# Snapshot of product 1 moved to the second accumulation bank, and half of the low parts to VectorE, in a folded feed-forward block

## The chip, the cores and the metric

The kernel runs on one core of a Trainium2 chip. The metric is device time in microseconds, the median of several runs. The engines are named as in the profile: PE (TensorE, matmuls), PEld (its weight loads, which overlap), DVE (VectorE), ACT (ScalarE), POOL (GpSimd) and SP (SyncE, which issues most DMAs here). Each engine works through its own queue in order; an instruction that waits for a semaphore holds back everything behind it on that engine.

## The reference

One step of a decoder layer on 520 tokens (512 of a new sequence and 8 single ones), all in fp32:

```python
def _swiglu(x, wg, wu, wd):
    return (jax.nn.silu(x @ wg) * (x @ wu)) @ wd

h = h + 0.5 * _swiglu(_rms_norm(h, ffn1_norm), ffn1_w_gate, ffn1_w_up, ffn1_w_down)   # FFN1
m, ... = _hybrid_mixer(_rms_norm(h, mix_norm), ...)     # pooling, convolution, SSD scan
h = h + m
h = h + 0.5 * _swiglu(_rms_norm(h, ffn2_norm), ffn2_w_gate, ffn2_w_up, ffn2_w_down)   # FFN2
return _rms_norm(h, final_norm), ...                    # and the new states
```

The model width is 1024, the hidden width of each feed-forward block 2816 = 22 x 128. Only FFN1 is touched by the change.

## The kernel before, in words

**Precision.** Each fp32 operand is split into a high part (`hi`, a cast on ACT to the type that TensorE multiplies) and a low rest (`lo` = x - hi). A product of two operands is three matmuls (`mm3`, lines 133, 136 and 137: hi.hi, hi.lo, lo.hi). A low part of weights is made in one of two ways: on DVE as one subtraction from the raw weights (`split` and `part`), or by `part_by_dma` (lines 218 to 220): ACT casts hi, ACT writes -hi into lo, and a DMA issued on POOL adds the raw weights from DRAM onto it.

**Seven products.** The token dimension is split into two halves of 260 and the weights into 2 x 2 blocks, and the four block products of a tile are replaced by seven products of sums (a fast scheme of the Strassen kind). `sums` builds the weight sums s1 (line 396) and s2 (lines 397 and 398) on DVE, each 128 x 1024, and splits them into `shi`/`slo` (c from s1, d from s2; casts at line 121, low parts at line 123). Products 1 and 2 use the plain weights `whi`/`wlo`, products 7 and 5 the c sums, 6 and 3 the d sums, and product 4 the quarter `qhi`/`qlo` (512 columns). One product is 4 x 3 = 12 matmuls of 128 x 128 by 128 x 260, and a tile of 7 products has 84.

**PSUM.** Each tile has one bank `A` and a pair of banks `BE`, both with two buffers. Products 1, 6, 7 and 4 run into `A`, each but the first on top of what is there; between them ACT takes snapshots of the running sum into SBUF (`ac`, line 456: product 1 to a[0], 6 to a[1], 7 to c[0]). Products 5 and 3 run into BE[1] (product 5 also is snapshotted, to c[1]), product 2 alone into BE[0]. `gates` then adds BE and a (line 473, 128 x 520), multiplies by the rms factor r (line 474), applies silu on ACT (line 475) and multiplies by the other half (line 476); `close` (line 488) uses A after product 4, and `keep_g` (lines 332 to 340) makes the pair sums of two gate tiles and splits them for the down projection.

**The stream.** `stream` runs over tiles 2 to 21 of gate and up weights, and after tiles 8 and 16 over four down tiles each (`Down(c, d)`): 28 tiles. Per tile it loads the raw weights (2 x 512 KB on SP, into `raw`, two buffers), makes the parts, and issues product 1, then product 4 and the close of the tile before, then 5, 6, 3, 7, 2 (tiles 2 and 21: 2, 5, 6, 3, 7), then `gates`. The plain weights `whi`/`wlo` and the sums' parts have two buffers each, the quarter one. In tiles 4 to 21 and in the down tiles wlo is made by `part_by_dma`; the quarter of tiles 2 to 20 too.

**What sets the order.** The kernel is written for a framework that orders each engine's instructions itself by its own estimate, respecting dependencies. Only where the code says so is the written order kept: `keep_in_program_order` on the first matmul of a product (`pin`; before the change product 7 of tile 2 and product 1 of tile 3), and `queued(...)`, which sets an instruction behind another. Elsewhere the products of neighbouring tiles interleave: product 5 of a tile before product 4 of the one before, for example, and product 2 before product 7. Buffers come free by semaphores, whole tile by whole tile.

After the stream comes a last down projection of tiles 16 to 21, then the mixer and FFN2, which is not folded in this way and keeps its own code paths.

Of the kernel before, what the change touches and what calls it, by code (L numbers as in the profile page):

```python
# [10 lines left out]
F32 = mybir.dt.float32  # L11
F32R = mybir.dt.float32r
AF = mybir.ActivationFunctionType
ALU = mybir.AluOpType
# [49 lines left out]
def tile_trunk_step(ctx: ExitStack, tc: tile.TileContext, ins: dict, outs: dict):  # L64
# [27 lines left out]
    def queued(*ins):  # L92
        stack = ExitStack()
        for i in ins:
            stack.enter_context(tc.issue_after(i))
        return stack
# [120 lines left out]
    def part_by_dma(hi, lo, s, home):  # L217
        nc.scalar.copy(hi, s)
        nc.scalar.activation(out=lo, in_=hi.bitcast(F32), func=AF.Copy, scale=-1.0)
        nc.gpsimd.dma_start(out=lo, in_=home, accum_op=ALU.add)  # L220
# [22 lines left out]
    class Ffn:  # L243
# [4 lines left out]
        def __init__(self, nx, i, wx, gp, direct):  # L248
            self.nx, self.i, self.wx, self.gp, self.direct = nx, i, wx, gp, direct
            self.states = None  # L250
            self.folded = CHUNKS[0] + CHUNKS[1] if i == 1 else 0
            self.held = {} if self.folded else {CHUNKS[0] + 1: None, CHUNKS[0] + CHUNKS[1] + 1: None}
            self.dram, self.gs, self.pairs, self.few, self.later = {}, {}, {}, [], []
            self.w, self.A, self.BE, self.ac, self.g, self.tg, self.raw, self.banks, self.behind, self.plain_kept = (
                {} for _ in range(10)
            )
# [98 lines left out]
        def load(self, f, first, then, by_dma):  # L355
            i, wx, src = self.i, self.wx, ins[f"w{self.i}gu"]
            n = f"{i}_{f}"
            raw = raw_pair(n)
            if isinstance(f, int):
                drams = [src[2 * f + u] for u in range(2)]  # L360
            else:
                lo = f.c * CHUNKS[0]
                drams = [ins[f"w{i}d"][2 * f.d + u, :, lo * P : (lo + 8) * P] for u in range(2)]
            self.dram[f] = drams
            for u in range(2):
                nc.sync.dma_start(out=raw[:, u], in_=drams[u])
            with queued(*first):
                if self.folded and (f, 0) not in LOW_ON_DVE:
                    d1 = weight_homes(1024, f"{n}a", wp, 3, ("whi", "wlo"))
                    part_by_dma(*d1, raw[:, 0], drams[0])  # L370
                else:
                    d1 = split(raw[:, 0], 1024, f"{n}a", wp, 3, ("whi", "wlo"))
            with queued(*then, *(ends if by_dma and i == 1 else ())):
                self.sums(f, n, src, raw, d1, by_dma)
# [39 lines left out]
        def quarter(self, f, src):  # L414
            n = f"{self.i}_{f}b"
            if self.folded:
                hi, lo = (self.wx.tile([P, 512], F32R, tag=t, name=f"{t}_{n}") for t in ("qhi", "qlo"))
                h, l = hi, lo
                if len(src.shape) == 3:
                    h, l = (t.rearrange("p (j c) -> p j c", j=4) for t in (hi, lo))  # L420
                if isinstance(f, int) and (f, 1) not in LOW_ON_DVE:
                    home = self.dram[f][1]
                    home = home[:, 512:] if isinstance(f, int) else home.rearrange("p (j q c) -> p q j c", q=2, c=P)[:, 1]
                    part_by_dma(h, l, src, home)
                else:
                    part(h, l, src)
                self.w[f][4] = (hi, lo), range(4)
                return
            self.w[f][4] = split(src, 512, n, wp, 3, ("whi", "wlo")), range(4)

        def product(self, f, p):
            js = range(KD // 2)
            if f not in self.A:
                self.load(f, *self.behind.get(f, ((), (), False)))
                n = f"{self.i}_{f}"
                self.A[f] = ps[0].tile([P, 512], F32, tag="A", bufs=2, name=f"A{n}")
                self.BE[f] = ps[0].tile([P, 2, 512], F32, tag="BE", bufs=2, name=f"BE{n}")
                self.ac[f] = [self.wx.tile([P, 2, HB], F32, tag="ac", bufs=3, name=f"ac{n}_{q}") for q in range(2)]
            if p != 1 and 4 not in self.w[f]:
                self.quarter(f, self.held[f])  # L440
            slot, dst, opens = {1: (0, 0, True), 2: (1, 1, True), 5: (3, 2, True), 6: (5, 0, False),
                                3: (2, 2, False), 7: (4, 0, False), 4: (6, 0, False)}[p]
            out = self.A[f] if dst == 0 else self.BE[f][:, dst - 1]
            (whi, wlo), k = self.w[f][p]
            xth, xtl = self.nx[:2]
            for j in js:
                if isinstance(f, int):
                    x = xth[:, j, slot], xtl[:, j, slot]
                else:
                    x = (self.gs[f.c * CHUNKS[0] // 2 + j][:, q, {5: 6, 6: 5}.get(slot, slot)] for q in range(2))  # L450
                mm3(out[:, :HB], ws(whi, k[j]), ws(wlo, k[j]), *x, opens and j == 0,
                    j == KD // 2 - 1, pin=j == 0 and (f, p) in ((2, 7), (3, 1)), skip_group_check=True)
            a, c = self.ac[f]
            keep = {1: a[:, 0], 6: a[:, 1], 7: c[:, 0], 5: c[:, 1]}.get(p)
            if keep is not None:
                nc.scalar.copy(keep, out[:, :HB])  # L456
            if p == 7:
                nc.vector.tensor_tensor(out=c[:, 0], in0=c[:, 0], in1=c[:, 1], op=ALU.add)

        def gates(self, f):  # L460
            if not isinstance(f, int):
                td = self.nx[2].rearrange("p (b t) -> p b t", b=2)
                r = self.nx[3].rearrange("p (b t) -> p b t", b=2)
                hd = h[:, 2 * f.d].rearrange("p (b t) -> p b t", b=2)
                a, c = self.ac[f]
                nc.vector.tensor_tensor(out=td, in0=self.BE[f][:, :, :HB], in1=a, op=ALU.add)
                nc.vector.scalar_tensor_tensor(out=td, in0=td, scalar=-0.5, in1=r, op0=ALU.mult, op1=ALU.mult)
                nc.vector.tensor_tensor(out=hd, in0=td, in1=hd, op=ALU.add)
                nc.vector.scalar_tensor_tensor(out=c[:, 1], in0=c[:, 0], scalar=0.5, in1=r[:, 1], op0=ALU.mult,
                                               op1=ALU.mult)  # L470
                return
            tg = self.tg[f] = self.gate_home(f)
            nc.vector.tensor_tensor(out=tg, in0=self.BE[f][:, :, :HB], in1=self.ac[f][0], op=ALU.add)
            nc.vector.tensor_tensor(out=tg, in0=tg, in1=self.nx[3].rearrange("p (b t) -> p b t", b=2), op=ALU.mult)
            nc.scalar.activation(out=tg, in_=tg, func=AF.Silu)
            nc.vector.tensor_tensor(out=tg[:, 1], in0=self.ac[f][1][:, 0], in1=tg[:, 1], op=ALU.mult)

        def close(self, f):
            if not isinstance(f, int):
                r = self.nx[3].rearrange("p (b t) -> p b t", b=2)  # L480
                hd = h[:, 2 * f.d + 1].rearrange("p (b t) -> p b t", b=2)
                c = self.ac[f][1]
                nc.vector.scalar_tensor_tensor(out=c[:, 0], in0=self.A[f][:, :HB], scalar=0.5, in1=r[:, 0],
                                               op0=ALU.mult, op1=ALU.mult)
                nc.vector.tensor_tensor(out=hd, in0=c, in1=hd, op=ALU.add)
                return
            tg = self.tg[f]
            nc.vector.tensor_tensor(out=tg[:, 0], in0=self.A[f][:, :HB], in1=tg[:, 0], op=ALU.mult)
            self.keep_g(f, tg)
# [4 lines left out]
        def stream(self, before, last_chunk):  # L494
# [6 lines left out]
            for t in tiles:  # L501
                self.product(t, 1)
                if prev is not None:
                    self.product(prev, 4)
                    self.close(prev)
                for p in (2, 5, 6, 3, 7) if t in (2, KF - 1) else (5, 6, 3, 7, 2):
                    self.product(t, p)
                self.gates(t)
                if t == 3:
                    with queued(*ends[1:]):  # L510
                        self.later.pop()()
                prev = t
# [150 lines left out]
    room = [*ffn1.cells("x2"), *ffn1.cells("x1"), *ffn1.cells("x0")]  # L663
    spare = [t.bitcast(F32) for t in ffn1.cells("sq")]
    sqs = spare.pop().rearrange("p (a b) t -> p a (b t)", a=2)
    ffn1.pairs[2] = spare.pop()

    def cell1(name):
        return room.pop().bitcast(F32)
# [723 lines left out]
```

## Time and profile before

| | before |
| --- | --- |
| time, median of 3 runs | 991.24 us (986.99, 991.24, 991.29) |
| profiled execution, its own time | 986.47 us |
| its span | 984.5 us, mean granted clock 0.995 |
| PE busy | 966.0 us (98%) |
| DVE busy | 815.6 us (83%) |
| ACT busy | 605.4 us (61%) |
| POOL busy | 125.7 us (13%) |
| moved by DMA | 135.18 MB, of it 29.63 MB on POOL's queue |

The time of the profiled execution is 2 us longer than its span, which begins and ends with the first and last instruction recorded. Matmuls are pipelined: a matmul row lasts 0.28 us, but the next one starts 0.12 us later, so a "busy" PE need not be one at its peak; the count of matmuls in a stretch tells more than the busy time. In the rows, `[1.75 <-ACT ac L456]` means that the engine was idle for 1.75 us before the instruction, and that an ACT instruction of line 456 on `ac` ended it. `SPq` and `POOLq` are DMA queues. A number behind a tile's name is its tile in the stream, and a letter the part: a plain, b quarter, c and d the two sums.

### The profile page before, as it was taken

How to read it: one execution, taken by the hardware profiler on the slowest of the kernel's cores; microseconds unless marked ns; L12 is line 12 of the kernel's file. 1: busy time of each engine (PE TensorE's matmuls, PEld its weight loads, DVE VectorE, ACT ScalarE, POOL GpSimd, SP SyncE). 2: the span in 40 equal slices, each digit the busy share in tenths (PEclk: the TensorE clock that was granted, in tenths of full speed). 3: DMA queues.
4: the chain of work that ended last, by engine and by line, in shares of the span. 5: the costliest groups of instructions: out<-in, count | busy, mean ns of one | idle time of the engine just before them, and what ended most of it. 6: DMA issues, size and time to landing. Idle time of an engine off the chain costs nothing.

```text
span 984.5 us, 19586 instructions
## 1 busy us (share of the span) xinstructions
PE 966.0 (98%) x7772; PEld 944.8 (96%) x7772; DVE 815.6 (83%) x1340; ACT 605.4 (61%) x1112; POOL 125.7 (13%) x206
## 2 busy tenths in 40 slices
PE   9999999999999999999999999999999999999996
PEld 8899999999989999999999999999999999999995
DVE  6898987888877688879978897999967899667886
ACT  7778657777557465485776675666643566514663
POOL 0011101111111000056341000100012000110010
PEclk9999999999999999999999999999999999999998
DMA  7577666776567232253334232523346423462232
GB/s 208 162 187 175 150 169 164 169 196 150 133 175 175 97 124 87 92 195 129 108 139 158 73 137 87 154 101 129 115 119 187 160 89 126 123 176 80 86 119 87
DMA packets 50459, 135.18 MB, mean 137 GB/s; under 512 B 7288, under 2 KB 15416, under 8 KB 50368
## 3 DMA queue, kind: packets, MB, share of 16 engines
q1 hardware_dynamic: 39840, 104.18, 30.8%
q0 software_dynamic: 10256, 29.63, 15.7%
q8 instruction: 61, 1.00, 0.4%
q14 instruction: 30, 0.25, 0.1%
q10 hardware_dynamic: 272, 0.13, 0.0%
HBM read 126.57 MB, written 7.34 MB: 136 GB/s over the span
## 4 chain that ended last, share of the span: by engine, by line
PE 78%; DVE 7%; DMA 7%; ACT 4%; issue 3%; SPq 0%; DVEq 0%; ACTq 0%
PE A L133 7%; PE A L136 7%; PE A L137 7%; PE BE L137 5%; PE BE L136 5%; PE BE L133 5%; PE P L282 4%; PE dn L137 4%; PE dn L136 4%; PE dn L133 4%; DMA raw<-in_w1gu 4%; PE wo L133 2%; PE wo L137 2%; PE wo L136 2%; PE inx L133 2%
## 5 line engine op out<-in xcount | busy, mean ns | idle before, releaser
L137 PE MATMUL dn<-g,wlo_2d 128*128 128x260 f32 x256 | 72.5, 283 | 0.0
L133 PE MATMUL dn<-g,whi_2d 128*128 128x260 f32 x256 | 72.1, 282 | 0.0
L136 PE MATMUL dn<-g,whi_2d 128*128 128x260 f32 x256 | 72.1, 282 | 0.0
L396 DVE TENSOR_TENSOR s<-raw 128x1024 f32<-128x1024 f32 x39 | 47.6, 1220 | 22.0 <-DMA raw<-in_w1gu 18.8
L456 ACT COPY ac<-A 128x260 f32<-128x260 f32 x123 | 44.0, 372 | 17.7 <-PE A L137 16.9
L133 PEld LDWEIGHTS dn<-g,whi_2d 128*128 128x128 f32 x256 | 48.2, 188 | 0.0
L136 PEld LDWEIGHTS dn<-g,whi_2d 128*128 128x128 f32 x256 | 48.2, 188 | 0.0
L137 PEld LDWEIGHTS dn<-g,wlo_2d 128*128 128x128 f32 x256 | 48.1, 188 | 0.0
L582 DVE SCALAR_TENSOR_TENSOR td<-dn,r_f 128x520 f32<-128x520 f32 (+1 forms) x25 | 16.8, 675 | 32.5 <-PE dn L137 32.5
L1121 POOL DMA_DIRECT2D out_nss<-hs x16 | 8.7, 545 | 259.1 <-DVE hs L1119 259.0
L121 ACT CAST whi_2d<-raw_2d 128x1024 fp32r<-128x1024 f32 (+1 forms) x18 | 18.5, 1026 | 36.8 <-PE dn L136 15.0
L133 PE MATMUL wo<-catg,whi_wo 128*128 128x260 f32 x128 | 37.1, 290 | 0.0
L133 PE MATMUL inz<-xh_mx,whi_inz 128*128 128x260 f32 x128 | 36.6, 286 | 0.0
L133 PE MATMUL inx<-xh_mx,whi_inx 128*128 128x260 f32 x128 | 36.4, 284 | 0.0
L137 PE MATMUL wo<-catg,wlo_wo 128*128 128x260 f32 x128 | 36.3, 283 | 0.0
L136 PE MATMUL inz<-xl_mx,whi_inz 128*128 128x260 f32 x128 | 36.2, 283 | 0.0
L137 PE MATMUL inz<-xh_mx,wlo_inz 128*128 128x260 f32 x128 | 36.2, 283 | 0.0
L136 PE MATMUL inx<-xl_mx,whi_inx 128*128 128x260 f32 x128 | 36.1, 282 | 0.0
L137 PE MATMUL inx<-xh_mx,wlo_inx 128*128 128x260 f32 x128 | 36.1, 282 | 0.0
L136 PE MATMUL wo<-catg,whi_wo 128*128 128x260 f32 x128 | 36.1, 282 | 0.0
L968 DVE SCALAR_TENSOR_TENSOR A<-U,h,A 128x544 f32<-128x544 f32 x36 | 28.8, 801 | 2.2 <-ACT A L966 1.8
L1117 ACT ACTIVATE so<-br,sxdt 128x128 f32<-128x128 f32 x64 | 20.4, 391 | 16.3 <-DMA br<-scr_bc 9.6
(2135 smaller groups left out, 4384.1 us busy)
## 6 DMA issues: line engine op xcount, KB each, us to landing
raw<-in_w2gu SPq DMA_DIRECT2D x44, 512.0 KB, 4.4
raw<-in_w1gu SPq DMA_DIRECT2D x41, 512.0 KB, 5.4
raw_2d<-in_w2d SPq DMA_DIRECT2D x16, 512.0 KB, 4.6
raw_wo<-in_w_out SPq DMA_DIRECT2D x12, 512.0 KB, 4.4
ab<-scr_acs SPq DMA_DIRECT2D x8, 512.0 KB, 3.7
h<-in_state_ssm SPq DMA_DIRECT2D x16, 256.0 KB, 3.2
raw_inz<-in_w_in SPq DMA_DIRECT2D x8, 512.0 KB, 4.4
hs<-in_state_ssm POOLq DMA_DIRECT2D x16, 256.0 KB, 3.4
```

Source lines behind the costliest of these rows:

```text
L121: cast = nc.scalar.copy(h, src)
L133: first = nc.tensor.matmul(ps, whi, xhi, start=start, stop=False, **kw)
L136: nc.tensor.matmul(ps, whi, xlo, start=False, stop=False, **kw)
L137: nc.tensor.matmul(ps, wlo, xhi, start=False, stop=stop, **kw)
L282: mm = nc.tensor.matmul(self.banks[f, u][b][:, :HB], ws(self.raw[f][:, u], j + 4 * q), xg[:, slot[q]], start=j == q == 0, stop=j == 3 and ...
L396: nc.vector.tensor_tensor(out=s1, in0=diag, in1=up0, op=ALU.add)
L456: nc.scalar.copy(keep, out[:, :HB])
L582: nc.vector.scalar_tensor_tensor(out=o, in0=s, scalar=-0.5, in1=q, op0=ALU.mult, op1=ALU.mult)
L968: nc.vector.scalar_tensor_tensor(out=A[:, :n], in0=U[:, j : j + n], scalar=w(j), in1=A[:, :n], op0=ALU.mult, op1=ALU.add)
L1117: nc.scalar.activation(out=o[:, q], in_=br, func=AF.Copy, scale=sxdt[:, j, b : b + 1]))
L1121: tc.keep_in_program_order(nc.gpsimd.dma_start(out=outs["nss"][:, b, 4 * g : 4 * g + 4], in_=hs))
```

## The change

Three things are edited, all for FFN1.

1. *Snapshot.* In all tiles but tile 2, the snapshot of product 1 is copied by ACT from bank A into bank BE[0] instead of into SBUF, and product 2 then accumulates on top of it, where before it opened the bank. The sum of BE and a in `gates` is then only needed in the second half (260 columns instead of 520) and is written in place in PSUM; the product with r reads from there.
2. *Low parts.* In tiles 4 to 21 the first 512 columns of wlo are subtracted on DVE; ACT and the accumulating DMA make only the second 512 columns. The quarter is made by the DMA only up to tile 6; from tile 7 on it is subtracted on DVE. The down tiles stay as they are.
3. *Order.* The first matmul of every product of FFN1 is pinned to the written order. The close of the tile before is issued after the first product of this tile that follows product 4, and silu is issued with the close, behind the last snapshot copy issued. The kept gates of an early tile (`later`) are closed at tile 5 instead of 3, and pair 4 gets a home in a spare cell.

```diff
--- before.py
+++ after.py
@@ -248,6 +248,7 @@
         def __init__(self, nx, i, wx, gp, direct):
             self.nx, self.i, self.wx, self.gp, self.direct = nx, i, wx, gp, direct
             self.states = None
+            self.whole = (2,)
             self.folded = CHUNKS[0] + CHUNKS[1] if i == 1 else 0
             self.held = {} if self.folded else {CHUNKS[0] + 1: None, CHUNKS[0] + CHUNKS[1] + 1: None}
             self.dram, self.gs, self.pairs, self.few, self.later = {}, {}, {}, [], []
@@ -367,7 +368,13 @@
             with queued(*first):
                 if self.folded and (f, 0) not in LOW_ON_DVE:
                     d1 = weight_homes(1024, f"{n}a", wp, 3, ("whi", "wlo"))
-                    part_by_dma(*d1, raw[:, 0], drams[0])
+                    hi, lo = d1
+                    n2 = 512 if isinstance(f, int) else 0
+                    nc.scalar.copy(hi, raw[:, 0])
+                    nc.scalar.activation(out=lo[:, n2:], in_=hi[:, n2:].bitcast(F32), func=AF.Copy, scale=-1.0)
+                    nc.gpsimd.dma_start(out=lo[:, n2:], in_=drams[0][:, n2:], accum_op=ALU.add)
+                    if n2:
+                        nc.vector.tensor_tensor(out=lo[:, :n2], in0=raw[:, 0, :n2], in1=hi[:, :n2].bitcast(F32), op=ALU.subtract)
                 else:
                     d1 = split(raw[:, 0], 1024, f"{n}a", wp, 3, ("whi", "wlo"))
             with queued(*then, *(ends if by_dma and i == 1 else ())):
@@ -418,7 +425,7 @@
                 h, l = hi, lo
                 if len(src.shape) == 3:
                     h, l = (t.rearrange("p (j c) -> p j c", j=4) for t in (hi, lo))
-                if isinstance(f, int) and (f, 1) not in LOW_ON_DVE:
+                if isinstance(f, int) and f <= 6 and (f, 1) not in LOW_ON_DVE:
                     home = self.dram[f][1]
                     home = home[:, 512:] if isinstance(f, int) else home.rearrange("p (j q c) -> p q j c", q=2, c=P)[:, 1]
                     part_by_dma(h, l, src, home)
@@ -440,6 +447,7 @@
                 self.quarter(f, self.held[f])
             slot, dst, opens = {1: (0, 0, True), 2: (1, 1, True), 5: (3, 2, True), 6: (5, 0, False),
                                 3: (2, 2, False), 7: (4, 0, False), 4: (6, 0, False)}[p]
+            opens = opens and (p != 2 or self.i == 2 or f in self.whole)
             out = self.A[f] if dst == 0 else self.BE[f][:, dst - 1]
             (whi, wlo), k = self.w[f][p]
             xth, xtl = self.nx[:2]
@@ -449,13 +457,24 @@
                 else:
                     x = (self.gs[f.c * CHUNKS[0] // 2 + j][:, q, {5: 6, 6: 5}.get(slot, slot)] for q in range(2))
                 mm3(out[:, :HB], ws(whi, k[j]), ws(wlo, k[j]), *x, opens and j == 0,
-                    j == KD // 2 - 1, pin=j == 0 and (f, p) in ((2, 7), (3, 1)), skip_group_check=True)
+                    j == KD // 2 - 1, pin=j == 0 and ((f, p) in ((2, 7), (3, 1)) or self.i == 1), skip_group_check=True)
             a, c = self.ac[f]
+            if p == 1 and self.i == 1 and f not in self.whole:
+                a = self.BE[f][:, :, :HB]
             keep = {1: a[:, 0], 6: a[:, 1], 7: c[:, 0], 5: c[:, 1]}.get(p)
             if keep is not None:
-                nc.scalar.copy(keep, out[:, :HB])
+                self.copied = nc.scalar.copy(keep, out[:, :HB]).ins
             if p == 7:
                 nc.vector.tensor_tensor(out=c[:, 0], in0=c[:, 0], in1=c[:, 1], op=ALU.add)
+
+        def sum(self, f, home=None):
+            be, a = self.BE[f][:, :, :HB], self.ac[f][0]
+            if self.i == 2:
+                nc.vector.tensor_tensor(out=home, in0=be, in1=a, op=ALU.add)
+                return home
+            s = slice(0, 2) if f in self.whole else slice(1, 2)
+            nc.vector.tensor_tensor(out=be[:, s], in0=be[:, s], in1=a[:, s], op=ALU.add)
+            return be
 
         def gates(self, f):
             if not isinstance(f, int):
@@ -463,16 +482,21 @@
                 r = self.nx[3].rearrange("p (b t) -> p b t", b=2)
                 hd = h[:, 2 * f.d].rearrange("p (b t) -> p b t", b=2)
                 a, c = self.ac[f]
-                nc.vector.tensor_tensor(out=td, in0=self.BE[f][:, :, :HB], in1=a, op=ALU.add)
-                nc.vector.scalar_tensor_tensor(out=td, in0=td, scalar=-0.5, in1=r, op0=ALU.mult, op1=ALU.mult)
+                be = self.sum(f)
+                nc.vector.scalar_tensor_tensor(out=td, in0=be, scalar=-0.5, in1=r, op0=ALU.mult, op1=ALU.mult)
                 nc.vector.tensor_tensor(out=hd, in0=td, in1=hd, op=ALU.add)
                 nc.vector.scalar_tensor_tensor(out=c[:, 1], in0=c[:, 0], scalar=0.5, in1=r[:, 1], op0=ALU.mult,
                                                op1=ALU.mult)
                 return
             tg = self.tg[f] = self.gate_home(f)
-            nc.vector.tensor_tensor(out=tg, in0=self.BE[f][:, :, :HB], in1=self.ac[f][0], op=ALU.add)
-            nc.vector.tensor_tensor(out=tg, in0=tg, in1=self.nx[3].rearrange("p (b t) -> p b t", b=2), op=ALU.mult)
-            nc.scalar.activation(out=tg, in_=tg, func=AF.Silu)
+            nc.vector.tensor_tensor(out=tg, in0=self.sum(f, tg), in1=self.nx[3].rearrange("p (b t) -> p b t", b=2), op=ALU.mult)
+            if self.i == 2:
+                self.silu(f)
+
+        def silu(self, f):
+            tg = self.tg[f]
+            with queued(*(() if self.i == 2 else (self.copied,))):
+                nc.scalar.activation(out=tg, in_=tg, func=AF.Silu)
             nc.vector.tensor_tensor(out=tg[:, 1], in0=self.ac[f][1][:, 0], in1=tg[:, 1], op=ALU.mult)
 
         def close(self, f):
@@ -484,6 +508,8 @@
                                                op0=ALU.mult, op1=ALU.mult)
                 nc.vector.tensor_tensor(out=hd, in0=c, in1=hd, op=ALU.add)
                 return
+            if self.i == 1:
+                self.silu(f)
             tg = self.tg[f]
             nc.vector.tensor_tensor(out=tg[:, 0], in0=self.A[f][:, :HB], in1=tg[:, 0], op=ALU.mult)
             self.keep_g(f, tg)
@@ -502,11 +528,12 @@
                 self.product(t, 1)
                 if prev is not None:
                     self.product(prev, 4)
-                    self.close(prev)
-                for p in (2, 5, 6, 3, 7) if t in (2, KF - 1) else (5, 6, 3, 7, 2):
+                for k, p in enumerate((2, 5, 6, 3, 7) if t in (2, KF - 1) else (5, 6, 3, 7, 2)):
+                    if k == 1 and prev is not None:
+                        self.close(prev)
                     self.product(t, p)
                 self.gates(t)
-                if t == 3:
+                if t == 5:
                     with queued(*ends[1:]):
                         self.later.pop()()
                 prev = t
@@ -663,7 +690,7 @@
     room = [*ffn1.cells("x2"), *ffn1.cells("x1"), *ffn1.cells("x0")]
     spare = [t.bitcast(F32) for t in ffn1.cells("sq")]
     sqs = spare.pop().rearrange("p (a b) t -> p a (b t)", a=2)
-    ffn1.pairs[2] = spare.pop()
+    ffn1.pairs[2], ffn1.pairs[4] = spare
 
     def cell1(name):
         return room.pop().bitcast(F32)
```

## The prediction

> **What bounds the kernel now.** I read the page's head first, then a table by windows, then TensorE's waits inside the first feed-forward block (FFN1), then the timelines of the engines that release those waits.
>
> ```profile
> span 984.5 us, 19586 instructions
> PE 966.0 (98%) x7772; PEld 944.8 (96%) x7772; DVE 815.6 (83%) x1340; ACT 605.4 (61%) x1112; POOL 125.7 (13%) x206
> ```
> ```profile
> 34.00:324.00 290.00, 282.40 (x2295) 278.77 (x2295) 241.43 (x352) 199.21 (x311) 37.80 (x45) 0.99 0.67 166
> ```
> ```profile
> 75.00:100.00 25.00, 25.00 (x210) 25.00 (x209) 21.37 (x32) 19.99 (x33) 4.20 (x5) 1.00 0.76 165
> ...
> 150.00:175.00 25.00, 23.22 (x188) 22.63 (x188) 20.24 (x30) 17.34 (x29) 4.20 (x5) 1.00 0.65 155
> ...
> 275.00:300.00 25.00, 22.61 (x174) 22.27 (x173) 17.25 (x25) 16.72 (x26) 3.35 (x4) 0.93 0.64 160
> 290.00:295.00 5.00, 4.64 (x26) 4.64 (x27) 4.91 (x9) 3.28 (x8) 1.07 (x2) 0.68 0.82 176
> ```
> The columns of the window rows are length, busy time (count) of PE, PEld, DVE, ACT and POOL, granted clock, DMA share and GB/s. TensorE is the bound: an undisturbed 25 us holds 210 matmuls, so one costs 0.119 to 0.120 us and a tile of 84 costs 10.06 us. No matmul is added or removed, so the change can only move the time in which TensorE stands still, and the order listings show that outside FFN1 nothing moves. FFN1's streamed tiles fill 34 to 324 us; 2295 x 0.1196 = 274.5 us, so at most 15.5 us of the 290 are lost (fewer, if matmul records are missing).
>
> TensorE's named waits in that stretch (total, times, longest):
>
> ```profile
> PE A L133 <- ACT ac L456: 4.9, 3, 2.4
> PE A_Down(c=1, d=1)_2849 L133 <- ACT ac_Down(c=1, d=1)_1_2852 L456: 1.2, 1, 1.2
> PE A_Down(c=0, d=1)_1314 L133 <- ACT ac_Down(c=0, d=1)_1_1317 L456: 0.5, 1, 0.5
> PE A_Down(c=1, d=2)_2973 L133 <- ACT ac_Down(c=1, d=2)_1_2976 L456: 0.3, 1, 0.3
> PE A_Down(c=0, d=3)_1562 L137 <- DVE slo_Down(c=0, d=3)d L123: 0.2, 1, 0.2
> ```
> Together 7.1 us, and nearly all one kind: product 4 of the previous tile, whose A bank must first be emptied by the copy of product 7 (L456). The timelines tell why that copy is late:
>
> ```profile
> 155.22 1.05 ACT L121 CAST shi_10c<-s 128x1024 fp32r<-128x1024 f32 x1 [0.69 <-PE BE L136]
> 159.42 1.05 ACT L218 CAST whi_11a<-raw 128x1024 fp32r<-128x1024 f32 x1 [3.15 <-DMA raw<-in_w1gu]
> 160.50 1.06 ACT L219 ACTIVATE wlo_11a<-whi_11a 128x1024 fp32r<-128x1024 f32 x1
> 161.47 1.03 ACT L121 CAST shi_10d<-s 128x1024 fp32r<-128x1024 f32 x1
> 162.40 0.64 ACT L456 COPY ac<-A 128x260 f32<-128x260 f32 x2
> ```
> ```profile
> 160.79 0.28 PE L137 MATMUL BE<-xth_f,slo_10c 128*128 128x260 f32 x1
> 162.82 0.39 PE L133 MATMUL A<-xth_f,qhi_9b 128*128 128x260 f32 x1 [1.75 <-ACT ac L456]
> ...
> 287.69 0.28 PE L137 MATMUL BE<-xth_f,slo_18c 128*128 128x260 f32 x1
> 290.36 0.39 PE L133 MATMUL A<-xth_f,qhi_17b 128*128 128x260 f32 x1 [2.39 <-ACT ac L456]
> ```
> ScalarE's queue is in order. whi_11a waited 3.15 us for tile 11's raw load, and tile 10's shi and tile 9's copy stood behind it; the PE rows show 2.03 us where 0.12 belong, and 2.67 us at the second place. After that second gap the clock is 0.68 (row 290 to 295): 26 matmuls where 5.00/0.1196 = 42 belong, 1.9 us, of which the end of the wait is 0.4. The Trainium skill, page TensorE: Matmul & The Clock Gate, Part 1, puts the fall to half clock behind an idle window of about 3.4 us; here a gap of 2.67 us sufficed, and the one of 2.03 us did not, so the measurement decides.
>
> **The change, part by part.** How late a raw load is, I read from its issue on SP and the first sum that needs both halves:
>
> ```profile
> 112.45 0.80 SPq L366 DMA_DIRECT2D raw_Down(c=0, d=2)_1413<-in_w1d  x2
> ...
> 152.71 0.85 SPq L366 DMA_DIRECT2D raw<-in_w1gu  x2
> ```
> ```profile
> 117.55 1.23 DVE L396 TENSOR_TENSOR s_Down(c=0, d=2)_1421<-raw_Down(c=0, d=2)_1413 128x1024 f32<-128x1024 f32 x1 [0.94 <-DMA raw_Down(c=0, d=2)_1413<-in_w1d]
> ...
> 161.75 1.23 DVE L396 TENSOR_TENSOR s<-raw 128x1024 f32<-128x1024 f32 x1 [3.61 <-DMA raw<-in_w1gu]
> ```
> ```profile
> wlo_10a<-in_w1gu POOLq DMA_DIRECT2D x1, 512.0 KB, 5.2
> ...
> qlo_10b<-in_w1gu POOLq DMA_DIRECT2D x1, 256.0 KB, 6.5
> ```
> Beside one accumulating transfer (a Down tile) a pair took 5.1 us; beside two (wlo and qlo on GpSimd's queue) 9.0 us. This is the row on which the rest turns.
>
> *Low parts.* Eighteen wlo transfers shrink from 512 to 256 KB and fourteen qlo transfers of 256 KB go: 18 x 0.26 + 14 x 0.26 = 8.4 MB less read, and 14 GpSimd issues fewer; ScalarE's preparation halves or goes. So the 9.0 us case loses its cause for tiles 7 to 20. I take 5 us for a landing, with 5.1 and 9.0 as the ends. VectorE gets 32 subtractions of 128x512, priced by L398, and 27 sums drop from 520 to 260 columns:
>
> ```profile
> L398 DVE TENSOR_TENSOR s<-s,raw 128x512 f32<-128x512 f32 x20 | 13.7, 683 | 0.1
> L473 DVE TENSOR_TENSOR gq<-BE,ac 128x520 f32<-128x520 f32 x17 | 11.8, 695 | 0.6
> L474 DVE TENSOR_TENSOR gq<-gq,r_f 128x520 f32<-128x520 f32 x17 | 11.8, 693 | 0.0
> L456 ACT COPY ac<-A 128x260 f32<-128x260 f32 x58 | 20.0, 371 | 3.6 <-PE A L137 3.6
> ```
> Back to back, instructions overlap, so starts count, not durations:
>
> ```profile
> 163.50 1.22 DVE L123 TENSOR_TENSOR slo_10d<-s,shi_10d 128x1024 fp32r<-128x1024 f32 x1
> 164.64 0.42 DVE L458 TENSOR_TENSOR ac<-ac 128x260 f32<-128x260 f32 x1
> 164.98 0.68 DVE L397 TENSOR_TENSOR s<-s,raw 128x512 f32<-128x512 f32 x1
> 165.58 0.42 DVE L476 TENSOR_TENSOR gq<-ac,gq 128x260 f32<-128x260 f32 x1
> ...
> 167.93 0.96 DVE L224 TENSOR_TENSOR gs<-gq,gs 128x780 fp32r<-128x780 f32 x1
> 168.81 0.69 DVE L224 TENSOR_TENSOR gs<-acc_f,gs 128x520 fp32r<-128x520 f32 x1
> 169.42 0.42 DVE L338 SCALAR_TENSOR_TENSOR gq<-gq 128x260 f32<-128x260 f32 x1
> ```
> 1024 columns hold VectorE 1.14 us, 780 0.88, 520 0.61, 512 0.60, 260 0.34. The change adds 32 x 0.60 - 27 x 0.27 = +11.9 us of VectorE work to the 241.4 of the stretch. It is hidden if VectorE keeps pace. In the changed order two tiles (12 and 13) give it thirty instructions: 6 of 1024, 1 of 780, 5 of 520, 8 of 512 and 10 of 260, which is 6.84 + 0.88 + 3.05 + 4.80 + 3.40 = 19.0 us, against TensorE's 20.12. Cover: 1.1 us per two tiles, 94% full. Between the subtraction that frees a raw buffer and the sum that needs its refill stand 5.5 us of work, so a landing above 5.5 us eats the cover, and above about 6.0 us TensorE starts to pay twice the excess per two tiles. At 5.1 us it costs nothing.
>
> *Snapshot into the second bank.* The same count of 128x260 copies; only the destination is PSUM. No row shows ScalarE writing PSUM: the nearest is the 371 ns copy from the same bank, which I take; ends 0.29 (its start interval) and 0.64 (the two-copy row at 162.40). A sum written in place into PSUM, and a product with r read from there, are taken at the equal 0.69 of L473, which reads PSUM, and L474, which does not. The Trainium skill, page Perfetto Trace Analysis, section Optimizing Scalar/DVE Operations, gives VectorE 125 ns per access to PSUM against 60 to SBUF; by it the 27 products with r would take 27 x 0.065 = 1.8 us more, an estimate; the 695 against 693 ns do not bear it out for reads. The new wait: product 5 may not start before the copy of product 1 is done. Between them stands product 4 of the previous tile, 12 x 0.12 = 1.44 us, less the copy: about 1.0 us of slack. Behind it in ScalarE's queue stand whi and the half wlo (1.05 + 0.62).
>
> *Order.* In the listing, the copy of product 7 and both shi of a tile now stand ahead of the whi that waits for the next raw, and product 4 follows product 1 directly. The stalls quoted lose their cause; late next is the copy of product 1, which stands behind that whi: with a first half landed by about 6 us it is in time. The close of a tile now comes after product 1 of the next; at four places (tiles 12, 14, 16 and Down 0,1) the next use of that A bank follows without slack, one 260 instruction of 0.34 us each: 1.2 us. SP's issues move with the release of raw, now by VectorE's subtraction some 4 to 5 us into the next tile where ScalarE's cast did it at about 5: no price. Later silu and the gates of pair 0: work off TensorE's path, no price while VectorE's cover holds.
>
> **Sum.** Recoverable between 8.6 (7.1 named + 1.5 clock) and 15.5; I take 12, the middle. The third of the three waits of 4.9 us, 4.9 - 2.4 - 1.75 = 0.7, belongs to the first tile, whose quarter still goes by transfer, and stays: 11.3 gained. Lost are 1.2 at the closes and 2 for the copies of product 1 (ends 0 and 6.4, the old waits in a new place). Net -8 us: the profiled 986.5 us would be 978.5. That run is the low end of the three shown (986.99 to 991.29, median 991.24); carried to the median: 983.
>
> **Rivals.**
> (a) No measurable change: the late raw stalls the copy of product 1 instead. For it speaks that whi still stands ahead of a copy; against it that the landing should be 5 us. At 0.3 us a tile (the wait of Down 1,2) 27 tiles give the 8 us back: 991, or 987 to 996 for 0.15 to 0.5 a tile.
> (b) Slower: VectorE becomes the bound of FFN1. For it: 94% full, and this row:
>
> ```profile
> DVE s L396 <- DMA raw<-in_w1gu: 18.8, 13, 4.3
> ```
> VectorE waits 18.8 us for raw loads today, 1.4 a time, and has little left to make it up. Decides from a landing of 6.0 us; at 7.0 each two tiles lose 2 x (7.0 - 6.0) = 2.0 us, over 18 tiles 18 us less the 8 gained: 1001. At 6.5, 992. Against: the queue beside the load carries under half of what made 9.0 us. The same section of the Trainium skill advises moving work off a saturated VectorE; the change does the reverse, and the row of 18.8 us bears this out only in part, since that is waiting, not work.
> (c) A larger gain: all 15.5 us go, nothing new: 976.
> (d) The halved sum does nothing by itself, the order all: same time as the forecast; VectorE's idle time is then unchanged by the 27 x 0.27 us.
>
> **How the numbers follow.** The forecast's own range is 977 to 987 (net 4 to 14): 0.61. Rival (a) 0.18, (b) 0.17, (c) 0.04. Half a per cent, about what a measurement here can tell, is 5 us: faster below 986.3. The forecast and (c) make 0.64 faster, (a) with the forecast's edge 0.18 same, (b) 0.18 slower. The range reaches from 975 to 998, leaving out the worst of (b).
>
> **What would show it.** Right: no wait of product 4 on L466 (the copy's new line) over 1 us, granted clock 1.00 from 34 to 324, raw landing near 5 us, VectorE about 87% busy there, and 2295 matmuls in about 282 us. Wrong: waits of product 5 on a copy, whi rows over 2 us ahead of it, or slo of VectorE as TensorE's main releaser, with VectorE above 93%.

## The result, and the profile after

The changed kernel takes 977.64 us (median of 4, 976.68 to 978.69) against 989.12 us (median of 4, the three runs shown ahead of the prediction and one of 986.93): ratio 0.9888, 95% interval 0.9869 to 0.9907. Faster, as forecast, by 11 us (1.1%) where 8 were forecast; the time lies in the range. The profiled execution took 978.69 us, against 986.47 us before.

The head of the page of the changed kernel, and FFN1's stretch by windows (columns as in the prediction):

```profile
span 976.9 us, 19565 instructions
PE 962.3 (99%) x7772; PEld 942.0 (96%) x7772; DVE 825.3 (84%) x1372; ACT 592.2 (61%) x1098; POOL 113.5 (12%) x192
```
```profile
34.00:324.00 290.00, 286.53 (x2358) 283.85 (x2357) 253.46 (x389) 188.74 (x303) 26.06 (x31) 1.00 0.53 142
```
The same 290 us now hold 2358 matmuls where they held 2295: 63 x 0.1196 = 7.5 us, nearly the whole 7.6 us by which the span is shorter. The clock is 1.00, the DMA share 0.53 instead of 0.67, VectorE 12.0 us busier. The transfers in that stretch, the raw loads and GpSimd's queue:

```profile
q0 software_dynamic: 4464, 10.23, 21.8%
...
raw<-in_w1gu SPq DMA_DIRECT2D x38, 512.0 KB, 4.5
```
GpSimd's queue (`q0`) moves 10.2 MB where it moved 18.6, and the median raw half lands in 4.5 us where it took 5.4. TensorE's waits in FFN1, the counterpart of the 7.1 us of before:

```profile
PE BE L133 <- ACT BE L466: 1.2, 2, 0.7
PE BE_Down(c=1, d=2)_2976 L133 <- ACT BE_Down(c=1, d=2)_2976 L466: 1.0, 1, 1.0
PE A L133 <- ACT ac L466: 0.5, 1, 0.5
PE BE_Down(c=0, d=2)_1441 L133 <- ACT BE_Down(c=0, d=2)_1441 L466: 0.2, 1, 0.2
```
Product 4's wait (the third row) is left at the first tile only. What is left elsewhere, 2.4 us, is a new kind: product 5, which needs BE, waits for the copy of product 1 into BE. The largest one, on ScalarE's and on TensorE's timeline:

```profile
250.79 1.05 ACT L373 CAST whi_Down(c=1, d=3)a<-raw_Down(c=1, d=3)_3074 128x1024 fp32r<-128x1024 f32 x1 [1.58 <-DMA raw_Down(c=1, d=3)_3074<-in_w1d]
251.87 1.06 ACT L374 ACTIVATE wlo_Down(c=1, d=3)a<-whi_Down(c=1, d=3)a 128x1024 fp32r<-128x1024 f32 x1
252.84 0.37 ACT L466 COPY BE_Down(c=1, d=2)_2976<-A_Down(c=1, d=2)_2975 128x260 f32<-128x260 f32 x1
```
```profile
252.01 0.28 PE L137 MATMUL A_Down(c=1, d=1)_2851<-gs,qlo_Down(c=1, d=1)b 128*128 128x260 f32 x1
253.26 0.39 PE L133 MATMUL BE_Down(c=1, d=2)_2976<-gs,shi_Down(c=1, d=2)c 128*128 128x260 f32 x1 [0.97 <-ACT BE_Down(c=1, d=2)_2976 L466]
```
A whi waits for raw, and the copy stands behind it: the chain of before, with another copy at its end. The operations that no row of before priced stand in the groups of the stretch:

```profile
L492 DVE TENSOR_TENSOR gq<-BE,r_f 128x520 f32<-128x520 f32 x16 | 11.1, 693 | 0.0
L476 DVE TENSOR_TENSOR BE<-BE,ac 128x260 f32<-128x260 f32 x19 | 8.2, 430 | 4.0 <-PE BE L137 4.0
...
L466 ACT COPY BE<-A 128x260 f32<-128x260 f32 x19 | 7.0, 366 | 1.8 <-PE A L137 1.8
```
The copy to PSUM takes 366 ns (371 to SBUF), the product with r 693 from PSUM as from SBUF, the sum in place 430. So the change is cheap instruction by instruction; which of its three parts brings the time is another question, for the experiments.

### The profile page after: what moved, and what is told of

It reads as the page before. It is cut to its first block, busy times and chain, and to the rows that moved or that the text cites. A ratio compares the mean times of both kernels' runs of the same rounds, so it can differ in the third digit from the quotient of the medians.

```text
span 976.9 us, 19565 instructions
## 1 busy us (share of the span) xinstructions
PE 962.3 (99%) x7772; PEld 942.0 (96%) x7772; DVE 825.3 (84%) x1372; ACT 592.2 (61%) x1098; POOL 113.5 (12%) x192
## 4 chain that ended last, share of the span: by engine, by line
PE 68%; DVE 3%; DMA 1%; issue 1%; ACT 0%; DVEq 0%; SPq 0%; ACTq 0%
PE A L137 5%; PE A L133 5%; PE A L136 5%; PE dn L137 4%; PE dn L133 4%; PE dn L136 4%; PE BE L137 4%; PE BE L136 4%; PE BE L133 4%; PE wo L133 2%; PE wo L137 2%; PE wo L136 2%; PE inx L133 2%; PE inz L133 2%; PE inz L136 2%; PE inz L137 2%
## 5 line engine op out<-in xcount | busy, mean ns | idle before, releaser
L466 ACT COPY ac<-A 128x260 f32<-128x260 f32 x104 | 38.5, 372 | 31.1 <-PE A L137 29.4
L466 ACT COPY ac<-BE 128x260 f32<-128x260 f32 x41 | 15.4, 375 | 26.9 <-PE BE L137 18.5
```

What stands on the lines that cost most here:

```text
L466: self.copied = nc.scalar.copy(keep, out[:, :HB]).ins
```

## The experiments

Each kernel was compared with the kernel before on the same chip. The three parts are called order, low parts and snapshot. The diffs are cut to the lines that matter, with `...` and comments for what is left out; they are against the changed kernel, that of the snapshot alone against the kernel before.

**Order alone.** Pins and places of close and silu as changed, the other two parts undone.

```diff
-                    if n2: nc.vector.tensor_tensor(out=lo[:, :n2], ...)      # and the half-width DMA
+                    part_by_dma(*d1, raw[:, 0], drams[0])
-                if isinstance(f, int) and f <= 6 and (f, 1) not in LOW_ON_DVE:
+                if isinstance(f, int) and (f, 1) not in LOW_ON_DVE:
-            if p == 1 and self.i == 1 and f not in self.whole:
-                a = self.BE[f][:, :, :HB]
```


> Only the order of the change (pins, close and silu moved); snapshot and low parts as before. Theory (order): the stalls come from the copy of product 7 standing behind a whi that waits for raw; with the copy ahead of it they go even if landings stay at 5 to 9 us: about 980 us, no wait of product 4 above 1 us, PE waits in FFN1 under 3 us. Rival (landing): the late raw is the cause wherever the copy stands, so the wait moves to product 6 or 1: 986 to 990.

Measured: 991.35 us, ratio 1.0034 (1.0017 to 1.0050): slower by a third of a per cent. Neither the theory (980) nor the rival (986 to 990, by a late raw load) foresaw what came. TensorE's waits, the first three rows and the one for ScalarE, from the list of thirteen:

```profile
PE A L137 <- DMA wlo_16a<-in_w1gu: 1.9, 1, 1.9
PE A L137 <- DMA wlo_10a<-in_w1gu: 1.4, 1, 1.4
PE A L137 <- DMA qlo_17b<-in_w1gu: 1.3, 1, 1.3
...
PE A L133 <- ACT ac L458: 1.0, 1, 1.0
```
Product 4 waits for a copy only at the first tile, so the order does what it should. Twelve waits for the accumulating transfers took the place: four for wlo, 5.0 us, and eight for qlo, 6.0 us (the expectation of a later run miscounts these as 6.0 and 5.6). GpSimd's issues, and how long these transfers took to land:

```profile
207.75 0.84 POOL L220 DMA_DIRECT2D wlo_15a<-in_w1gu  x1 [7.21 <-ACT wlo_15a L219]
211.59 0.83 POOL L220 DMA_DIRECT2D qlo_14b<-in_w1gu  x1 [3.00 <-PE BE L137]
220.80 0.84 POOL L220 DMA_DIRECT2D wlo_16a<-in_w1gu  x1 [8.38 <-ACT wlo_16a L219]
221.97 0.83 POOL L220 DMA_DIRECT2D qlo_15b<-in_w1gu  x1 [0.33 <-ACT qlo_15b L219]
```
```profile
wlo_15a<-in_w1gu POOLq DMA_DIRECT2D x1, 512.0 KB, 5.8
wlo_16a<-in_w1gu POOLq DMA_DIRECT2D x1, 512.0 KB, 8.7
...
qlo_14b<-in_w1gu POOLq DMA_DIRECT2D x1, 256.0 KB, 6.3
qlo_15b<-in_w1gu POOLq DMA_DIRECT2D x1, 256.0 KB, 9.3
```
Issued 3.8 us apart they land in 5.8 and 6.3 us; 1.2 us apart, in 8.7 and 9.3. In the fixed order wlo of a tile and qlo of the tile before become ready 1.2 to 1.4 us apart at tiles 10, 12, 14 and 16, the four whose wlo TensorE waits for.

**Low parts alone.** The edit of the low parts, with the free order and the old snapshot.

```diff
-                    j == KD // 2 - 1, pin=j == 0 and ((f, p) in ((2, 7), (3, 1)) or self.i == 1), ...)
+                    j == KD // 2 - 1, pin=j == 0 and (f, p) in ((2, 7), (3, 1)), ...)
-                for k, p in enumerate(...):            # close after the next product, silu in close
-                    if k == 1 and prev is not None:
-                        self.close(prev)
+                    self.close(prev)                   # right after product 4, silu in gates
```


> Only the low parts of the change; order and snapshot as before. Theory (order): the two 9 us landings shrink to about 5, and with them the two largest stalls (1.9 and 2.6 us and the half clock behind one), but copies of product 7 still stand behind whi: 983 to 986. Rival (landing): nearly the whole gain, 978 to 981. Rival (VectorE bound): slower than before, 990 or more, VectorE above 93% in FFN1.

Measured: 984.22 us, ratio 0.9952 (0.9937 to 0.9967). The first rows of TensorE's waits:

```profile
PE A L133 <- ACT ac L464: 1.8, 4, 0.7
PE A L137 <- DVE slo_4d L123: 1.3, 1, 1.3
PE A_Down(c=0, d=0)_1194 L133 <- ACT ac_Down(c=0, d=0)_1_1197 L464: 1.0, 1, 1.0
```
The two long stalls are gone and the clock of the stretch is 1.00; many short waits of the old kind stay. A gain of 4.5 us, not 11.

**Snapshot alone.** Product 1 copied to the second bank and the half sum, the other two parts undone.

```diff
+            if p == 1 and self.i == 1 and f not in self.whole:
+                a = self.BE[f][:, :, :HB]             # copied here, product 2 opens no bank
+            s = slice(0, 2) if f in self.whole else slice(1, 2)
+            nc.vector.tensor_tensor(out=be[:, s], in0=be[:, s], in1=a[:, s], op=ALU.add)
```


> Only the snapshot of product 1 in the second bank with the halved sum; order and low parts as before. Theory: VectorE is not on the path, so 27 x 0.27 us less there gives nothing, and product 2, which the order puts early, now waits for the copy: 988 to 993. Rival (the sum counts): 983 to 986.

Measured: 1020.98 us, ratio 1.0334 (1.0305 to 1.0363), far worse than expected. In the free order product 4 of a tile stands behind product 1 of the next; ScalarE's timeline at the longest wait:

```profile
190.08 1.05 ACT L121 CAST shi_12c<-s 128x1024 fp32r<-128x1024 f32 x1 [0.57 <-PE BE L136]
194.99 1.04 ACT L218 CAST whi_13a<-raw 128x1024 fp32r<-128x1024 f32 x1 [3.86 <-DMA raw<-in_w1gu]
196.07 1.06 ACT L219 ACTIVATE wlo_13a<-whi_13a 128x1024 fp32r<-128x1024 f32 x1
197.03 1.03 ACT L121 CAST shi_12d<-s 128x1024 fp32r<-128x1024 f32 x1
197.97 0.37 ACT L460 COPY ac<-A 128x260 f32<-128x260 f32 x1
...
198.77 0.38 ACT L460 COPY BE<-A 128x260 f32<-128x260 f32 x1
```
The same chain as before, whi ahead of the copy of product 7 (the row at 197.97). Before, product 5 of the next tile ran between its product 1 and product 4 of the tile before and covered part of that; now it needs BE, and the copy of product 1 into it (the last row) comes behind the copy of product 7.

**Low parts and snapshot, free order.** The changed kernel with the order undone, by the diff shown for the low parts alone.

> Low parts and snapshot as changed, the order free. Theory (the free order puts product 4 behind a late copy once product 2 has to wait for the copy of product 1, as with the snapshot alone, and the shorter landing takes out part): 990 to 1010. Rival (the 32 us of the snapshot alone came from the landing): 980 to 986.

Measured: 1002.43 us, ratio 1.0121 (1.0095 to 1.0146). TensorE still waits for that copy:

```profile
PE A L133 <- ACT ac L466: 10.4, 6, 3.9
```
With the shorter landing the 32 us of the snapshot alone shrink to 12; what TensorE still waits for is nearly all this copy (with two down tiles 15.0 us), which no kernel with the fixed order shows past its first tile.

**Order and low parts, no snapshot.** Run twice, the second time beside the changed kernel.

```diff
-            if p == 1 and self.i == 1 and f not in self.whole:
-                a = self.BE[f][:, :, :HB]
-            self.whole = (2,)
+            self.whole = (*range(KF), *(Down(c, d) for c in range(2) for d in range(KD // 2)))
```

> The change without its snapshot: product 1 is copied to SBUF, the sum is over 520 columns; order and low parts as changed. Theory: product 5 no longer waits for the copy of product 1 (2.6 us of waits in the changed kernel go), and VectorE has 7.3 us more work, hidden: 975 to 977. Rival (VectorE is nearly the bound and needs the halved sum): 980 to 986, TensorE waiting for slo.

> The changed kernel itself, beside the next run on the same chip. 977 to 979.

> The change without its snapshot once more. If the snapshot in the second bank costs time (product 5 waiting for the copy of product 1), 975 to 976.5 and outside the interval of the run beside it; if it is neutral, 977 to 979.

Measured: ratio 0.9879 (0.9851 to 0.9907) at first; then 977.70 us, 0.9855 (0.9839 to 0.9870), against 978.41 us, 0.9864 (0.9847 to 0.9880) for the changed kernel. TensorE's waits and the stretch of the second run without the snapshot:

```profile
PE A L137 <- DMA qlo_5b<-in_w1gu: 1.5, 1, 1.5
PE A L133 <- ACT ac L464: 0.7, 1, 0.7
```
```profile
34.00:324.00 290.00, 287.56 (x2381) 286.25 (x2380) 262.08 (x391) 189.22 (x304) 26.06 (x31) 1.00 0.54 142
```
The waits of product 5 are gone, and VectorE does 8 us more without TensorE noticing. By the times the snapshot is worth nothing that can be measured beside the other two parts: the intervals overlap. Order and snapshot without the low parts was not run.

**Which low part.** Order as changed, no snapshot, and only one of the two: half of wlo on VectorE with the quarter by transfer, or the quarter on VectorE with wlo of 1024 columns by transfer.

```diff
-                if isinstance(f, int) and f <= 6 and (f, 1) not in LOW_ON_DVE:    # half wlo alone
+                if isinstance(f, int) and (f, 1) not in LOW_ON_DVE:
```
```diff
-                    n2 = 512 if isinstance(f, int) else 0                         # quarter alone
+                    part_by_dma(*d1, raw[:, 0], drams[0])
```


> Order as changed and half of wlo on VectorE; the quarter still by the accumulating transfer, snapshot as before. The order alone left TensorE waiting 12.6 us for accumulating transfers: 6.0 us for wlo (five waits), 5.6 us for qlo (seven). Theory (each transfer's own landing is on the path): the wlo waits go, those for qlo stay: 983 to 986. Rival (only the shared landing counts): most of both go, 977 to 979.

> Order as changed and the quarter of tiles 7 to 20 on VectorE; wlo of 1024 columns by the accumulating transfer, snapshot as before. Theory (own landing): the qlo waits from tile 7 on go, those for wlo stay, smaller because one transfer fewer is in the queue: 980 to 985. Rival (only the sum of traffic counts): as with the half wlo alone.

Measured: 981.92 us, ratio 0.9916 (0.9890 to 0.9942), with the half wlo; 978.13 us, 0.9872 (0.9848 to 0.9895), with the quarter. First rows of TensorE's waits with the half wlo:

```profile
PE A L137 <- DMA qlo_17b<-in_w1gu: 2.2, 1, 2.2
PE A L137 <- DMA qlo_9b<-in_w1gu: 1.6, 1, 1.6
```
and a transfer with the quarter on VectorE:

```profile
wlo_16a<-in_w1gu POOLq DMA_DIRECT2D x1, 512.0 KB, 5.4
```
With the half wlo the waits for qlo stay, 7.0 us in five. With the quarter moved, wlo_16a lands in 5.4 us instead of 8.7 though it is no smaller, wlo of tiles 10, 12 and 14 in 5.6 to 5.7 instead of 7.8 to 8.5, and from tile 7 on no transfer is waited for. So the rule of the transfer's own landing holds for qlo, while wlo was late only through its neighbour. In the changed order the quarter alone brings what the whole change brings, within the intervals; the quarter with the free order was not run.

**whi behind the copy.** The changed kernel with whi of the next tile set behind this tile's copy of product 1.

```diff
+                if self.first_copy is not None:
+                    first = (*first, self.first_copy)      # first: what whi is issued after
+                self.load(f, first, then, by_dma)
```


> The changed kernel with the whi of the next tile set behind this tile's copy of product 1 into the second bank. Theory: the three waits of product 5 (2.4 us named, about 3 with the refill) come from that whi waiting for raw; they go: 974 to 976. Rival (the copy is late for other reasons): no change, 977 to 979; wlo comes too late: slower, 980 or more.

Measured: 1008.97 us, ratio 1.0187 (1.0161 to 1.0214). The waits of product 5 are gone and worse has come. ScalarE's rows of one down tile, and the wait it makes on TensorE:

```profile
127.10 1.05 ACT L374 CAST whi_Down(c=0, d=2)a<-raw_Down(c=0, d=2)_1415 128x1024 fp32r<-128x1024 f32 x1
129.25 0.62 ACT L223 CAST qhi_Down(c=0, d=1)b<-raw_Down(c=0, d=1)_1291 128x512 fp32r<-128x512 f32 x1 [1.10 <-issue]
129.78 1.06 ACT L375 ACTIVATE wlo_Down(c=0, d=2)a<-whi_Down(c=0, d=2)a 128x1024 fp32r<-128x1024 f32 x1
```
```profile
PE A_Down(c=0, d=2)_1440 L137 <- DMA wlo_Down(c=0, d=2)a<-in_w1d: 3.6, 1, 3.6
```
whi later means wlo and its transfer later, and all eight down tiles wait for it.

**All of wlo on VectorE.**

```diff
-LOW_ON_DVE = ((2, 0), (3, 0), (KF - 1, 1))
+LOW_ON_DVE = (*((f, 0) for f in range(2, KF)), (KF - 1, 1))
```


> The changed kernel with all 1024 columns of wlo of tiles 4 to 21 subtracted on VectorE, no accumulating transfer for them. VectorE gets 18 x 0.54 = 9.7 us more, 20.1 us of work per two tiles against TensorE's 20.12. Theory (VectorE nearly the bound, as in the second rival): TensorE starts to wait for slo, 981 to 990. Rival (VectorE has room, landing near 4.4 us): 976 to 979.

Measured: 993.24 us, ratio 1.0026 (1.0011 to 1.0042), some 15 us above the changed kernel and above the theory's range. Thirty microseconds by windows, with this edit and then twice in the changed kernel, and the largest of TensorE's waits with it:

```profile
150.00:180.00 30.00, 29.83 (x249) 29.63 (x248) 29.84 (x43) 16.97 (x30) 0.00 (x0) 1.00 0.35 123
```
```profile
64.00:94.00 30.00, 29.90 (x246) 29.52 (x246) 29.85 (x48) 22.50 (x39) 4.20 (x5) 1.00 0.56 133
150.00:180.00 30.00, 29.20 (x241) 28.79 (x240) 27.35 (x44) 18.99 (x31) 2.02 (x3) 1.00 0.48 132
```
```profile
PE A L133 <- DVE gq L514: 7.7, 2, 5.4
```
With the edit VectorE is busy 29.84 of 30 us and falls behind; TensorE does its 249 matmuls all the same and stops just after, when product 1 of tile 12 waits for a close (L514) in VectorE's queue. The busy share of one window does not tell the two cases apart: the changed kernel is as full between 64 and 94 us, and that stays hidden. Counted over 34 to 324 us, VectorE's work against the time that the matmuls done there need (count x 0.1196 us) is 0.90 in the changed kernel and 0.92 without the snapshot, both hidden, and 0.94 here. In the stretch TensorE does 114 matmuls fewer than in the changed kernel (2244 against 2358), 13.6 us. Three stalls on VectorE make up most of it, 3.12, 5.65 and 2.61 us from start to start, each followed by half clock for one or two times 3.41 us.

**Quarter of tiles 4 to 6 on VectorE too**, without the snapshot.

```diff
-                if isinstance(f, int) and f <= 6 and (f, 1) not in LOW_ON_DVE:
+                if isinstance(f, int) and f <= 3 and (f, 1) not in LOW_ON_DVE:
```

> The change without its snapshot, and the quarter of tiles 4 to 6 on VectorE too (by transfer only for tiles 2 and 3). Theory (a transfer's own landing is on the path): the wait of 0.46 us for qlo_4b and the 0.26 us at qlo_5b, with their refills about 1 us, go: 974 to 975.5. Rival (VectorE is full there, with the early gates): equal or slower than without this edit.

Measured: 979.12 us, ratio 0.9871 (0.9856 to 0.9887): no gain, as the rival said. The waits for qlo_4b and qlo_5b are gone, but TensorE waits 1.2 us for shi_6d and 0.8 us for slo_6d instead; by the count above VectorE stands at 0.93.

## Why the prediction was right, and where it was not

*What bounds it.* Confirmed: TensorE stood behind the copy of product 7, which stood behind a whi that waited for raw. All of the difference lies in FFN1.

*Low parts.* Confirmed in size: 12.0 us more VectorE work in the stretch against 11.9, 87% busy, and raw at 4.5 us (median of the halves, 5.4 before). But the row of 9.0 us was read too widely. In the kernel before, from 36 us on, the second raw half took 8.5 and 8.7 us at the two long stalls alone, where the load was issued 1.2 and 1.3 us behind a wlo transfer with a qlo right after it; with wlo 2.3 us or more ahead it took 4.5 to 6.5 us, qlo or not. And the reason given was half the truth. I costed the accumulating transfers only for what they do to the raw load beside them; that qlo is itself waited for by product 4, and that two of them 1.2 us apart delay each other to 8.7 and 9.3 us, is shown by the order alone and was in no term.

*Order.* "The stalls quoted lose their cause" holds (no kernel with the fixed order has a wait of product 4 on a copy past the first tile). "Late next is the copy of product 1" fails as a statement about the order: alone it makes the transfers late next, 11.0 us of waits, and is slower. The gain is not a sum: order +3 us, low parts -4.5, both together -13.

*Snapshot.* Priced right: 366 ns for the copy (371 taken), product with r at 693. The Trainium skill, page Perfetto Trace Analysis, section Optimizing Scalar/DVE Operations, gives VectorE some 65 ns more on PSUM; here 430 against 422 (L476 of before) and 693 against 693 do not agree. Product 5's waits, named as a sign of being wrong, did come; they were taken as 2 us and are 2.4. Rival (d) was right that the halved sum does nothing, wrong that the order does all.

*Closes.* The four places are there; TensorE's timeline of the changed kernel ahead of product 1 of tile 12:

```profile
177.45 0.28 PE L137 MATMUL BE<-xth_f,wlo_11a 128*128 128x260 f32 x1
177.80 0.39 PE L133 MATMUL A<-xth_f,whi_12a 128*128 128x260 f32 x1
```
0.35 us where 0.12 belong, and the next start 0.1 late as well: 0.33 us here, nearly the same at tiles 14, 16 and Down 0,1, 1.3 us in all against the 1.2 forecast.

*Rivals.* (a)'s mechanism came, at four places rather than 27. (b) did not come; 9.7 us more VectorE work than the change has made it bind. The sign named for it, VectorE above 93%, fails as a busy share: with all of wlo it is 253.49 of 290 us, 87% as in the changed kernel, since a stalled TensorE holds up VectorE's work too. As work against the time of the matmuls done, 0.92 is hidden and 0.94 is not.

*The sum.* 978.5 us forecast for the profiled execution, 978.69 measured. That it meets to 0.2 us is partly luck: the sum has no term for the 11.0 us of transfer waits that the order brings, and comes out because the low parts, priced for another reason, take them away. The step that failed is the one from there to the median: I added the 4.8 us by which the median of before stood above its profiled run. Over all runs on record the kernel before spread from 985.86 to 993.32 us and the changed one from 976.68 to 979.09, so the changed kernel lost the scatter as well. Why it scatters was not tested; a stall that sometimes trips the clock (below) is one candidate. The record leans that way without settling it: of the 19 runs of the kernel before beside the order alone, the six shortest have a granted clock of 0.996 to 0.997, and five of the six longest 0.993 to 0.995.

## What to carry to other kernels

A fixed order that brings a consumer forward needs the producer to be able to follow: price the landing of every transfer that the new neighbour waits for, not only the copies. Two parts that each gain little or lose can gain together, so test them as a square, not one at a time. And work hidden on a nearly full engine does not price the next piece: 9.7 us more of subtractions on VectorE cost 15 us, part of it in the half clock behind its three stalls.

## What the runs showed of the hardware

How long TensorE may pause before the clock falls. The gap is start to start in the PE timeline; each row is 3 us beginning 0.5 us after the gap (PEclk is the third figure from the end), first of the kernel before after gaps of 2.03 and 2.67 us:

```profile
163.32:166.32 3.00, 3.00 (x27) 2.99 (x26) 3.00 (x7) 2.09 (x4) 0.28 (x1) 1.00 0.92 168
290.86:293.86 3.00, 3.00 (x20) 3.00 (x19) 3.00 (x7) 2.07 (x4) 0.26 (x1) 0.65 0.97 168
```
then of the snapshot alone after 2.68 us, and of whi behind the copy after 2.21 and 2.92 us:

```profile
223.18:226.18 3.00, 3.00 (x28) 3.00 (x27) 3.00 (x7) 2.01 (x4) 0.29 (x1) 1.00 0.99 169
```
```profile
68.27:71.27 3.00, 3.00 (x16) 3.00 (x15) 3.00 (x6) 1.22 (x3) 0.00 (x0) 0.50 0.00 0
...
262.50:265.50 3.00, 3.00 (x16) 3.00 (x15) 0.76 (x2) 1.26 (x2) 0.00 (x0) 0.50 0.00 0
```
Of the 27 gaps from 1.86 us up in the stretch 34 to 324 us, in seven kernels, none of the four up to 2.03 us was followed by a fall, 7 of the 13 between 2.21 and 2.86 us were, and all ten from 2.92 to 5.65 us. Between 2.2 and 2.9 us the length of a gap does not decide. The Trainium skill, page TensorE: Matmul & The Clock Gate, Part 1, gives about 3.4 us; the rows show falls well below it.

What decides in between can be read from the clock record of the traces. In every run with more than one spell at half clock, the spells begin whole multiples of 3.413 us apart (in the snapshot alone at 92.38, 129.93, 198.19, 249.39 and 273.29 us), and those inside FFN1 last one or two such steps. Take from each of the 27 gaps, less 0.12 us for the matmul that opens it, the largest part that lies in one step: with up to 1.89 us none of 8 was followed by a fall, with 2.09 us or more all 15 were, and between, 2 of 4. So a gap of 2.21 us that lay inside one step was followed by half clock, and one of 2.86 us, of which 1.89 us lay in one step, was not.
